# FFN 2's input projection in Strassen's form: seven half-size products in place of eight, with its result kept in DRAM

## The chip, the cores and the metric

One core of a Trainium2 chip runs the whole program. The metric is device time in microseconds (us), the median of three runs. Engines: PE (TensorE: matmul), DVE (VectorE), ACT (ScalarE), POOL (GpSimd), SP (SyncE, which only starts DMAs here). Each engine works through its own instructions in a fixed order, and waits for others through semaphores.

## The reference

One step of a decoder layer on 1056 rows (1024 of a prompt, 32 of samples) with a model width of 1024. The change concerns the last of its three parts, the second FFN:

```python
D_MODEL, D_FF = 1024, 2816

def swiglu_ffn(h, w_in, w_out):
    a, b = jnp.split(h @ w_in, 2, axis=-1)
    return (jax.nn.silu(a) * b) @ w_out

def decoder_layer(...):
    ...                                            # first FFN
    x = x + gt2[:, None, :] * m                    # attention and retention, merged
    h = modulate(x, norm_ffn2, sh3, sc3)           # RMS norm, scale, shift
    x = x + HALF_STEP * gt3[:, None, :] * swiglu_ffn(h, ffn2_w_in, ffn2_w_out)
```

A final RMS norm over x gives the main output. All data are float32.

## The kernel before

Activations lie transposed in SBUF: feature k*128+p on partition p of tile k, the 1056 rows along the free axis, cut into three row blocks `rb` of 352 columns (the last one holds the 32 sample rows too). Every float32 operand of a large product is split in two parts, `h` (rounded) and `l` (the rest), by `split` (L176): ACT copies with rounding, DVE (or POOL, where a weight reader has `eng=G`) subtracts. A product of two such operands is three matmuls, h·h, h·l and l·h (`mm3`, L225 to L230), each with its own 128x128 weights. `hh[k]`, `hl[k]` (k = 0..7) are the split normed input of the part that runs, and `X` (named Y here) is the residual x.

The work is one long program: FFN 1, then retention and attention, the merged output projection `w_out` (matmuls into `wop`, L1321 to L1328), and FFN 2. What sets the order is the order in the code together with a list scheduler that places instructions on their engines; weights are read ahead by SP, as far as buffers are free.

FFN 2 is the call of `ffn` at L1376. The 2816 hidden features are 22 tiles `ft` of 128. `CHUNKS2` puts them in chunks of four (the last of two). For each tile of a chunk the weights `wa{ft}`, `wb{ft}` (1024x128 each) are read and split (one ACT and one DVE instruction of 1024 columns each); then for each row block `pa` = h·wa and `pb` = h·wb are made by 24 matmuls of 352 columns each (`unit`, L242), ACT takes silu of `pa` (L512), DVE multiplies by `pb` (L513), and the product is split into `gh`, `gl` (L514). After a chunk its output projection runs: for each of eight output tiles and three row blocks, 3 x (tiles of the chunk) matmuls of 352 columns into `po`, which DVE adds into x (`residual`, L481). So all of x and all of a chunk's `gh`, `gl` stay in SBUF.

`norm` (L449) for row blocks 0 and 1 runs between the last products of `w_out` (L1328), that of row block 2 inside FFN 2's first tile (`final`, L1331). Its last steps are the splits `hl`, by DVE for even k and by POOL for odd k (L473). At the end `after2` (L1341) makes the final norm and writes the output.

The instruction that the page calls `L179 ... x<-y,yh` is the subtraction of a split; `L172` is its rounding copy.

## Time and profile before

| | |
|---|---|
| median of three runs | 3204.2 us (3199.22 to 3204.82) |
| the profiled execution: its own time | 3204.28 us |
| its span, first to last instruction | 3202.5 us |
| mean granted TensorE clock | 0.986 of 2.4 GHz |
| busy PE / DVE / ACT / POOL | 96% / 53% / 36% / 14% |
| first matmul of FFN 2 / first of its tile 2 | 2412.55 us / 2466.59 us |

Times of rows are microseconds from the span's start. A PE row has the start of a matmul and how long it is in the pipe; since matmuls overlap, the distance between starts (called pitch below) says what one costs. "Idle before <-releaser" names what a late instruction waited for.

### The profile page before, as it was taken

The page shows a single profiled execution, that of the slowest core. Times are in us where ns is not written, and L with a number is a line of the kernel's source. Part 1 is how long each engine was busy: PE and PEld are TensorE (multiplying, and loading weights), DVE is VectorE, ACT ScalarE, POOL GpSimd, SP SyncE. Part 2 cuts the span into 40 slices and gives each one's busy share as a digit, 9 for nine tenths or more (in the row PEclk, how much of TensorE's full clock was granted, in tenths as well). Part 3 has the DMA queues.
Part 4 walks back from the last instruction along what each step waited for, and adds up shares of the span by engine and source line. Part 5 has one row for each costly group of instructions (what it writes and reads, how often), then busy time and mean ns, then how long its engine had stood idle before and what let it go on. Part 6 is the DMA issues. An engine that isn't in the chain of part 4 may idle for free.

```text
span 3202.5 us, 47920 instructions
## 1 busy us (share of the span) xinstructions
PE 3060.3 (96%) x19135; PEld 2925.4 (91%) x19135; DVE 1700.5 (53%) x3683; ACT 1151.3 (36%) x2164; POOL 452.0 (14%) x456
## 2 busy tenths in 40 slices
PE   7999999999999999999999998998999999999998
PEld 4999999999999999988888888988889999999998
DVE  6443434334366666668867777776655323233235
ACT  5422232222234243346555556554444111111113
POOL 2000000000132222212222222223021000000002
PEclk9999999999999999999999999998999999999999
DMA  6232222221131322222221121225622111111111
GB/s 215 61 116 81 80 91 87 86 79 53 52 121 59 100 77 83 89 84 84 75 65 60 56 71 56 73 68 172 202 74 66 47 46 47 47 47 47 47 47 61
DMA packets 261369, 254.18 MB, mean 79 GB/s; under 512 B 13216, under 2 KB 223649, under 8 KB 261146
## 3 DMA queue, kind: packets, MB, share of 16 engines
q1 hardware_dynamic: 245226, 200.38, 20.5%
q0 software_dynamic: 15920, 50.74, 4.5%
...
q14 instruction: 73, 0.60, 0.1%
...
## 4 chain that ended last, share of the span: by engine, by line
PE 39%; DVE 9%; ACT 3%; issue 1%; DMA 1%; POOL 0%; DVEq 0%; SPq 0%; ACTq 0%; POOLq 0%
PE pb L228 3%; PE pa L228 3%; PE pa L229 3%; PE pa L230 3%; PE pb L229 3%; PE pb L230 3%; PE po L228 3%; PE po L229 2%; PE po L230 2%; PE gp L228 1%; PE gp L230 1%; PE gp L229 1%; ACT P L1139 1%; PE at L1163 1%; DVE rao L334 1%
## 5 line engine op out<-in xcount | busy, mean ns | idle before, releaser
L513 DVE TENSOR_TENSOR silu<-silu,pb 128x352 f32<-128x352 f32 x132 | 68.7, 521 | 503.5 <-PE pb L230 501.4
L172 ACT ACTIVATE gh<-silu 128x352 fp32r<-128x352 f32 x132 | 65.2, 494 | 325.4 <-DVE silu L513 325.2
L484 DVE SCALAR_TENSOR_TENSOR Y<-po,mod,Y 128x352 f32<-128x352 f32 (+1 forms) x144 | 82.1, 571 | 123.3 <-PE po L230 123.2
L447 POOL TENSOR_TENSOR acc<-acc,sq 128x352 f32<-128x352 f32 x27 | 29.8, 1103 | 804.7 <-ACT sq L446 795.8
L484 DVE SCALAR_TENSOR_TENSOR X<-po,mod,X 128x352 f32<-128x352 f32 (+1 forms) x144 | 81.7, 570 | 112.1 <-PE po L230 111.6
L512 ACT ACTIVATE silu<-pa 128x352 f32<-128x352 f32 x132 | 60.5, 458 | 205.9 <-PE pa L230 205.8
L1139 ACT ACTIVATE P<-s,mx 128x256 f32<-128x256 f32 (+7 forms) x128 | 94.9, 742 | 80.4 <-DVE mx L1137 72.2
L447 POOL TENSOR_TENSOR accf<-accf,sq 128x352 f32<-128x352 f32 x9 | 8.8, 974 | 726.8 <-ACT sq L446 726.8
L228 PE MATMUL po<-gh,wo_0h 128*128 128x352 f32 x288 | 94.6, 328 | 5.1 <-DVE X L484 4.1
L1137 DVE TENSOR_REDUCE mx<-s 128x1 f32<-128x256 f32 (+7 forms) x128 | 95.5, 752 | 1.8
L229 PE MATMUL po<-gl,wo_0h 128*128 128x352 f32 x288 | 93.8, 326 | 0.0
L230 PE MATMUL po<-gh,wo_0l 128*128 128x352 f32 x288 | 93.7, 325 | 0.0
L179 DVE TENSOR_TENSOR gl<-silu,gh 128x352 fp32r<-128x352 f32 x132 | 69.1, 524 | 46.2 <-ACT gh L172 45.8
L228 PE MATMUL po<-gh,wo_1h 128*128 128x352 f32 x288 | 93.4, 324 | 0.0
L230 PE MATMUL po<-gh,wo_1l 128*128 128x352 f32 x288 | 92.8, 322 | 0.0
L229 PE MATMUL po<-gl,wo_1h 128*128 128x352 f32 x288 | 92.6, 322 | 0.0
L172 ACT ACTIVATE ah<-at 128x512 fp32r<-128x512 f32 (+1 forms) x80 | 44.4, 555 | 98.4 <-PE at L1163 97.7
L228 PE MATMUL po<-gh,wo_3h 128*128 128x352 f32 x240 | 77.5, 323 | 1.2 <-DVE rs L489 1.2
L228 PE MATMUL po<-gh,wo_2h 128*128 128x352 f32 x240 | 77.7, 324 | 0.0
L229 PE MATMUL po<-gl,wo_2h 128*128 128x352 f32 x240 | 77.2, 322 | 0.0
L229 PE MATMUL po<-gl,wo_3h 128*128 128x352 f32 x240 | 77.2, 322 | 0.0
L230 PE MATMUL po<-gh,wo_2l 128*128 128x352 f32 x240 | 77.2, 321 | 0.0
...
## 6 DMA issues: line engine op xcount, KB each, us to landing
...
```

Source lines behind the costliest of these rows:

```text
L172: S.activation(out, in_, AF.Copy, scale=scale)
L179: (eng or V).tensor_tensor(out=l, in0=src, in1=f(h), op=ALU.subtract)
L228: T.matmul(out, wh, xh, start=first and j == 0, stop=False)
L229: T.matmul(out, wh, xl, start=False, stop=False)
L230: behind[0] = T.matmul(out, wl_, xh, start=False, stop=last and j == n - 1).ins
L334: V.scalar_tensor_tensor(out=a[:, j:j + 1], in0=y[:, j:j + 1], scalar=y[:, j:j + 1], in1=h[:, j:j + 1], op0=ALU.mult, op1=ALU.mult)
L447: (V if k % 2 else G).tensor_tensor(out=acc[k % 2], in0=acc[k % 2], in1=sq[:], op=ALU.add)
L484: V.scalar_tensor_tensor(out=x[k][:, c0:c0 + n], in0=p_[:, :n], scalar=gt[:, k, 0:1], in1=x[k][:, c0:c0 + n], op0=ALU.mult, op1=ALU.add)
L512: S.activation(s_[:], pa[:, :RB], AF.Silu)
L513: V.tensor_tensor(out=s_[:], in0=s_[:], in1=pb[:, :RB], op=ALU.mult)
L1137: V.tensor_reduce(out=mx[:], in_=ss[:, :wd], op=ALU.max, axis=AX.X, negate=True)
L1139: S.activation(pt[:, :wd], ss[:, :wd], AF.Exp, bias=mx[:], accum_out=rs[:, c:c + 1])
```

## The change

Twenty of the 22 input tiles of FFN 2 (ft 2 to 21) are computed in Strassen's form (Winograd's variant). The input h is cut in four: features 0..511 and 512..1023 by columns 0..527 and 528..1055; the weights of one tile in four as well: wb and wa, each by its upper and lower 512 features. Instead of eight products of quarters there are seven, with sums of weight quarters (`s1` to `s4`) and of input quarters (`T1` to `T4`) as operands, and the four result quarters are put together from the seven products in PSUM and by DVE and ACT.

- A product is 4 (k) x 3 (h·h, h·l, l·h) x 2 (column halves `s` of 264) = 24 matmuls of 264 columns; a tile has 168 in place of 144 of 352.
- Input sums `T1` to `T3` are made once (`sums`), into new tiles `gx`; `T4` (`last_sum`) takes the place of h's upper right quarter. Each is split again.
- Per tile: seven splits of 512 columns, four sums of 512 on DVE, and ten evictions of 264 columns on each of DVE and ACT. Six PSUM banks, x, q and y times two halves, each single, hold the products: x collects the first, third, fifth and sixth product one upon the other and is read after each, q the fourth and seventh, y the second.
- A tile's product silu(a)·b isn't split into `gh`, `gl`, but stored to DRAM (`gd`, through POOL's queue), and read back at the output projection (`ffn_out`, `gr`, through SP's queue, two buffers) and split there into `hh`, `hl`, which are free by then.
- x is stored to DRAM after each row block of `w_out` (`keep`), since its SBUF is needed for `gx`, and read back (`Z`) ahead of the output projection, which now follows all 22 input tiles.
- Tiles 0 and 1 are made as before (`ffn_plain`), so that `sums` can be made beside them.
- Everywhere in the program, a split whose subtraction is POOL's is cut along its second axis in pieces of two: four of 256 columns for one of 1024.

```diff
     def split(h, l, src, scale=1.0, eng=None):
         acth(h, src, scale)
-        if isinstance(scale, float) and scale == 1.0:
+        if eng is G:
+            for a in range(0, h.shape[1], 2):
+                G.tensor_tensor(out=l[:, a:a + 2, :], in0=src[:, a:a + 2, :], in1=f(h)[:, a:a + 2, :], op=ALU.subtract)
+        elif isinstance(scale, float) and scale == 1.0:
             (eng or V).tensor_tensor(out=l, in0=src, in1=f(h), op=ALU.subtract)
...
+    def sums(ta, gx):
+        def less(a, b, tag, name):
...
+        for k in range(4):
+            b11, b12, b22 = half(k, 0), half(k, 1), half(4 + k, 1)
+            t1 = less(b12, b11, "p1", f"t1_{k}")
+            split(*(x[:] for x in gx[0][k]), t1[:])
+            yield
+            V.tensor_tensor(out=t1[:], in0=f(b22[0]), in1=t1[:], op=ALU.subtract)
+            V.tensor_tensor(out=t1[:], in0=t1[:], in1=f(b22[1]), op=ALU.add)
+            split(*(x[:] for x in gx[1][k]), t1[:])
+            yield
+            split(*(x[:] for x in gx[2][k]), less(b22, b12, "u2", f"t3_{k}")[:])
+            yield
...
+    def ffn_seven(w, ta, gx, win, fts, once, more=iter(()), per=0):
+        operand = [[half(k, 0) for k in range(4)], [half(4 + k, 0) for k in range(4)],
+                   *([(h[:], l[:]) for h, l in gx[c]] for c in (1, 0, 2)),
+                   [half(k, 1) for k in range(4)], [half(4 + k, 1) for k in range(4)]]
+        X_, Q_, Y_ = range(3)
+        home = (X_, Y_, X_, Q_, X_, X_, Q_)
+        opens = (0, 1, 3)
...
+            yield two(a11, "c1")
+            yield two(a12, "c2")
+            s1 = s_(a21, a22, ALU.add, "s1")
+            s2 = s_(s1, a11, ALU.subtract, "s2")
+            yield two(s2, "c6")
+            yield two(s1, "c5")
+            s4 = s_(a12, s2, ALU.subtract, "s4")
+            yield two(s_(a11, a21, ALU.subtract, "s3"), "c7")
+            yield two(a22, "c4")
+            yield two(s4, "c3")
...
+            for j in range(7):
...
+                for s in range(2):
+                    cs_ = slice(s * QR, (s + 1) * QR)
+                    mm3(p[home[j]][s][:, :QR], [(wh[:, k, :], wl_[:, k, :]) for k in range(4)],
+                        [(h[:, cs_], l[:, cs_]) for h, l in operand[j]], first=j in opens, skip_group_check=True)
+                for s in range(2):
...
+                    if j == 0:
+                        S.activation(p1[:, cs_], x, AF.Copy)
+                    elif j == 1:
+                        V.tensor_tensor(out=p1[:, cs_], in0=p1[:, cs_], in1=y, op=ALU.add)
+                    elif j == 2:
+                        S.activation(u2[:, cs_], x, AF.Copy)
+                    elif j == 3:
+                        S.activation(p5[:, cs_], q, AF.Copy)
+                    elif j == 4:
+                        V.tensor_tensor(out=p5[:, cs_], in0=p5[:, cs_], in1=x, op=ALU.add)
+                        S.activation(p5[:, cs_], p5[:, cs_], AF.Silu)
+                    elif j == 5:
+                        S.activation(sa[:, cs_], x, AF.Silu)
+                        V.tensor_tensor(out=p1[:, cs_], in0=p1[:, cs_], in1=sa[:, cs_], op=ALU.mult)
+                    else:
+                        V.tensor_tensor(out=u2[:, cs_], in0=u2[:, cs_], in1=q, op=ALU.add)
+                        V.tensor_tensor(out=u2[:, cs_], in0=u2[:, cs_], in1=p5[:, cs_], op=ALU.mult)
+                if j == 5:
+                    st(out=gd[ft][:, :HR], in_=p1[:])
+                elif j == 6:
+                    st(out=gd[ft][:, HR:], in_=u2[:])
+                next(once, None)
...
+    def ffn_out(w, tp, x, wout, gt, after, chunks, homes, bridge=iter(()), more=iter(())):
+        def stage(ci):
+            for q, ft in enumerate(chunks[ci]):
+                r = tp.tile([P, ROWS], F32, tag="gr", name=f"gr{ft}", bufs=2)
+                ld(out=r[:], in_=gd[ft][:, :])
+                split(*(t[:] for t in homes[ci][q]), r[:])
+                yield
...
+        def keep(rb):
+            st(out=xd[:, rbs(rb)].rearrange("(k p) c -> p k c", p=P), in_=X[:, :, rbs(rb)])
...
-            ffn(s2, w, pool(s2, "t2"), x, i["ffn2_w_in"][0], i["ffn2_w_out"][0], lambda: mods[8], after2, CHUNKS2, 1,
-                pre={(0, 0): final()})
+            todo = back()
+            win2 = i["ffn2_w_in"][0]
+            ffn_plain(w3, tp2, win2, [0, 1], 1, {(0, 0): final()}, todo)
+            for _ in todo:
+                pass
+            psum_seven(1)
+            ffn_seven(w3, gx[3], gx, win2, list(range(2, DFF // P)), last_sum(gx[3], gx))
...
+            ffn_out(w3, pool(s2, "t3"), x, i["ffn2_w_out"][0], lambda: mods[8], after2, CHUNKS2,
+                    [[(hh[c % 2 * 4 + q], hl[c % 2 * 4 + q]) for q in range(4)] for c in range(len(CHUNKS2))])
```

In the rows of the order below a weight name like `c12` is the split quarter sum c1 of tile 2 (`c621`: c6 of tile 21), both of its parts in one tile; `x2_0` is PSUM bank x of tile 2, column half 0.

**PE at the entry to tile 2.** Before, tile 1's last matmul (`wb1`) is followed by tile 2's first:

```order
L229 MATMUL pb1_2_24535<-hl7_121,wb1h_24396 128x352
L230 MATMUL pb1_2_24535<-hh7_113,wb1l_24397 128x352
L228 MATMUL pa2_0_24577<-hh0_106,wa2h_24567 128x352
L229 MATMUL pa2_0_24577<-hl0_114,wa2h_24567 128x352
L230 MATMUL pa2_0_24577<-hh0_106,wa2l_24568 128x352
L228 MATMUL pa2_0_24577<-hh1_107,wa2h_24567 128x352
```

With the change:

```order
L235 MATMUL pb1_2_24789<-hl7_143,wb1h_24641 128x352
L236 MATMUL pb1_2_24789<-hh7_135,wb1l_24642 128x352
L234 MATMUL x2_0_24865<-hh0_128,c12_24879 128x264
L235 MATMUL x2_0_24865<-hl0_136,c12_24879 128x264
L234 MATMUL x2_1_24866<-hh0_128,c12_24879 128x264
L235 MATMUL x2_1_24866<-hl0_136,c12_24879 128x264
L234 MATMUL y2_0_24869<-hh4_132,c22_24882 128x264
L235 MATMUL y2_0_24869<-hl4_140,c22_24882 128x264
L234 MATMUL y2_1_24870<-hh4_132,c22_24882 128x264
L235 MATMUL y2_1_24870<-hl4_140,c22_24882 128x264
L236 MATMUL x2_0_24865<-hh0_128,c12_24879 128x264
L234 MATMUL x2_0_24865<-hh1_129,c12_24879 128x264
```

Tile 2 now begins with the two matmuls that need only the rounded part, for each half of the first two products (c1, c2), and only then comes the l·h matmul (L236), which needs the subtracted part of c1.

**DVE from the end of the norm to that point.** Before, from the last `hl` of the norm on, two weight splits of 1024 columns and the work on tile 0 stand there:

```order
L513 TENSOR_TENSOR silu0_1_24328<-silu0_1_24328,pb0_1_24303 128x352
L476 SCALAR_TENSOR_TENSOR hl6_120<-nt2_6_24264,mod6_4694,hh6_112 128x352
L179 TENSOR_TENSOR gl0_24127<-silu0_1_24328,gh0_24123 128x352
L179 TENSOR_TENSOR wb1l_24397<-wb1r_24394,wb1h_24396 128x1024
L513 TENSOR_TENSOR silu0_2_24383<-silu0_2_24383,pb0_2_24358 128x352
L179 TENSOR_TENSOR wa2l_24568<-wa2r_24565,wa2h_24567 128x1024
L179 TENSOR_TENSOR gl0_24127<-silu0_2_24383,gh0_24123 128x352
L513 TENSOR_TENSOR silu1_0_24450<-silu1_0_24450,pb1_0_24425 128x352
```

With the change `hl6` of row block 2 is followed by 47 rows (42 of 528 columns for the input sums, one weight split of 1024, four `silu` products of 352) before c1 of tile 2, whose last ones are:

```order
L185 TENSOR_TENSOR gl03_24487<-t1_3_24843,gh03_24486 128x528
L572 TENSOR_TENSOR silu1_2_24814<-silu1_2_24814,pb1_2_24789 128x352
L601 TENSOR_TENSOR t1_3_24843<-hh7_135,t1_3_24843 128x528
L593 TENSOR_TENSOR t3_3_24854<-t3_3_24854,t3_3u_24855 128x528
L602 TENSOR_TENSOR t1_3_24843<-t1_3_24843,hl7_143 128x528
L185 TENSOR_TENSOR c12_24879<-wb2r_24875,c12_24879 128x512
L185 TENSOR_TENSOR gl23_24503<-t3_3_24854,gh23_24502 128x528
L185 TENSOR_TENSOR gl13_24495<-t1_3_24843,gh13_24494 128x528
```

The subtraction for `c12`, which had no such work ahead of it, now stands behind nearly all of `sums`.

**DVE within a tile.** Before, tile 17 to 18: 352-column products and splits, and one weight split of 1024 for each half of a tile's weights:

```order
L513 TENSOR_TENSOR silu17_0_28818<-silu17_0_28818,pb17_0_28793 128x352
L179 TENSOR_TENSOR gl1_24128<-silu17_0_28818,gh1_24124 128x352
L513 TENSOR_TENSOR silu17_1_28873<-silu17_1_28873,pb17_1_28848 128x352
L179 TENSOR_TENSOR gl1_24128<-silu17_1_28873,gh1_24124 128x352
L179 TENSOR_TENSOR wb18l_28942<-wb18r_28939,wb18h_28941 128x1024
L513 TENSOR_TENSOR silu17_2_28928<-silu17_2_28928,pb17_2_28903 128x352
L179 TENSOR_TENSOR wa19l_29113<-wa19r_29110,wa19h_29112 128x1024
L179 TENSOR_TENSOR gl1_24128<-silu17_2_28928,gh1_24124 128x352
L513 TENSOR_TENSOR silu18_0_28995<-silu18_0_28995,pb18_0_28970 128x352
```

With the change, from tile 20's second product to its sixth:

```order
L185 TENSOR_TENSOR c420_29150<-wa20r_28977,c420_29150 128x512
L185 TENSOR_TENSOR c320_29179<-s420_29117,c320_29179 128x512
L682 TENSOR_TENSOR p1_20_29113<-p1_20_29113,y20_0_29111 128x264
L644 TENSOR_TENSOR s421_29350<-wb21r_29208,s221_29274 128x512
L682 TENSOR_TENSOR p1_20_29113<-p1_20_29113,y20_1_29112 128x264
L185 TENSOR_TENSOR c121_29212<-wb21r_29208,c121_29212 128x512
L185 TENSOR_TENSOR c221_29241<-wb21r_29208,c221_29241 128x512
L185 TENSOR_TENSOR c621_29276<-s221_29274,c621_29276 128x512
L688 TENSOR_TENSOR p5_20_29115<-p5_20_29115,x20_0_29107 128x264
L644 TENSOR_TENSOR s321_29352<-wb21r_29208,wa21r_29210 128x512
L688 TENSOR_TENSOR p5_20_29115<-p5_20_29115,x20_1_29108 128x264
```

The addition of bank x to `p5` (L688), which frees that bank for the next product, now stands behind two or three splits of later weights.

**SP at the start of the output projection.** Before, an output chunk's weights stood between weights of input tiles:

```order
L197 DMA wb3r_24748<-ffn2_w_in 128x8x128
L197 DMA wo0_0r_24919<-ffn2_w_out 128x4x256
L197 DMA wo0_1r_25015<-ffn2_w_out 128x4x256
L197 DMA wo0_2r_25111<-ffn2_w_out 128x4x256
L197 DMA wo0_3r_25207<-ffn2_w_out 128x4x256
L197 DMA wa4r_25303<-ffn2_w_in 128x8x128
L197 DMA wb4r_25309<-ffn2_w_in 128x8x128
```

With the change:

```order
L203 DMA wb21r_29208<-ffn2_w_in 128x8x128
L203 DMA wa21r_29210<-ffn2_w_in 128x8x128
L203 DMA wo0_0r_29590<-ffn2_w_out 128x4x256
L203 DMA wo0_1r_29690<-ffn2_w_out 128x4x256
L203 DMA wo0_2r_29790<-ffn2_w_out 128x4x256
L203 DMA wo0_3r_29890<-ffn2_w_out 128x4x256
L709 DMA gr0_29574<-gd0_67 128x1056
L709 DMA gr1_29578<-gd1_68 128x1056
L203 DMA wo1_0r_29990<-ffn2_w_out 128x4x256
L709 DMA gr2_29582<-gd2_69 128x1056
L709 DMA gr3_29586<-gd3_70 128x1056
```

The readings of `gd2`, `gd3` wait until the first two buffers `gr` have been split, and stand ahead of all later loads.

## Rows read from the trace of the kernel before

**Rows 1.** From the page: busy time of the engines over the whole span (share of it, number of instructions), and the busy tenths of DVE in 40 slices of 80 us.

```profile
PE 3060.3 (96%) x19135; PEld 2925.4 (91%) x19135; DVE 1700.5 (53%) x3683; ACT 1151.3 (36%) x2164; POOL 452.0 (14%) x456
...
DVE  6443434334366666668867777776655323233235
```

**Rows 2.** Windows (from:to, length, then busy time and number of instructions of PE, PE weight loads, DVE, ACT and POOL, the granted clock, the DMA share and rate): two stretches of 100 us within FFN 2, and the last.

```profile
2500.00:2600.00 100.00, 100.00 (x631) 100.00 (x630) 32.65 (x62) 14.78 (x22) 0.00 (x0) 1.00 0.15 43
2900.00:3000.00 100.00, 100.00 (x630) 100.00 (x630) 33.91 (x64) 15.73 (x23) 0.00 (x0) 1.00 0.18 53
3100.00:3202.50 102.50, 91.40 (x590) 88.79 (x588) 48.30 (x126) 26.52 (x48) 18.79 (x17) 0.94 0.16 58
```

**Rows 3.** What PE waited for from 2440 us to the end (engine, line, releaser: us in all, times, longest).

```profile
PE yt L1363 <- ACT yo L1366: 2.3, 3, 1.8
PE ym L1356 <- POOL accf L447: 1.3, 1, 1.3
PE yt L1363 <- DVE rs L489: 0.4, 1, 0.4
PE pa L229 <- POOL hl L473: 0.3, 1, 0.3
```

**Rows 4.** PE timeline (start, us in the pipe, line, operands): the first matmul of `pa5_2` and the first of `pa6_1`, with the 96 matmuls of 352 columns from the one to the other.

```profile
2596.32 0.32 PE L228 MATMUL pa<-hh,wa5h 128*128 128x352 f32 x1
2611.58 0.32 PE L228 MATMUL pa<-hh,wa6h 128*128 128x352 f32 x1
```

**Rows 5.** PE timeline: the first and the thirteenth of thirteen successive matmuls of 256 columns in a retention chunk, then the first and the sixth of six of 288 columns in attention, all with weights of their own.

```profile
980.77 0.28 PE L228 MATMUL U<-vh,nh 128*128 128x256 f32 x1
...
982.19 0.28 PE L228 MATMUL pro<-ph,vh 128*128 128x256 f32 x1
...
2231.45 0.29 PE L228 MATMUL sc<-kth,qmh 128*128 128x288 f32 x1
...
2232.11 0.29 PE L230 MATMUL sc<-kth,qml 128*128 128x288 f32 x1
```

**Rows 6.** Groups of DVE instructions by line, operation and shape (count, then busy us, mean ns of one, then idle time before them and its releaser): subtractions and products of two float32 tiles of 352, 512, 1024 and 256 columns.

```profile
L513 DVE TENSOR_TENSOR silu<-silu,pb 128x352 f32<-128x352 f32 x132 | 68.7, 521 | 503.5 <-PE pb L230 501.4 <-ACT silu L512 2.1
L179 DVE TENSOR_TENSOR al<-at,ah 128x512 fp32r<-128x512 f32 x48 | 32.9, 686 | 19.4 <-ACT ah L172 19.4
L179 DVE TENSOR_TENSOR wo_1l<-wo_1r,wo_1h 128x1024 fp32r<-128x1024 f32 x12 | 14.7, 1226 | 20.5 <-ACT wo_1h L172 20.5
L561 DVE TENSOR_TENSOR gs<-nh 128x256 f32<-128x256 f32 x16 | 6.7, 422 | 7.4 <-ACT nh L560 7.4
```

**Rows 7.** The same for ACT: copies and squares of 512 and 256 columns.

```profile
L172 ACT ACTIVATE sth<-st 128x512 fp32r<-128x512 f32 x32 | 20.2, 631 | 85.5 <-PE srx L857 77.7 <-DMA st<-state_ret 7.7
L1175 ACT ACTIVATE osq<-o 128x256 f32<-128x256 f32 x32 | 12.2, 382 | 17.2 <-PE o L230 17.0
```

**Rows 8.** DVE timeline at the end of the norm of row block 2 and after it.

```profile
2439.03 0.57 DVE L476 SCALAR_TENSOR_TENSOR hl<-nt,mod,hh 128x352 fp32r<-128x352 f32 x1
2439.78 0.52 DVE L179 TENSOR_TENSOR gl<-silu,gh 128x352 fp32r<-128x352 f32 x1 [0.18 <-ACT gh L172]
```

**Rows 9.** PE timeline: tile 2's first matmul.

```profile
2466.59 0.32 PE L228 MATMUL pa<-hh,wa2h 128*128 128x352 f32 x1
```

**Rows 10.** PE timeline around the one long wait of PE in the `w_out` phase (from 2399.89 to 2402.06 six matmuls start), then the granted clock of the two windows behind it (columns as in rows 2).

```profile
2394.92 0.32 PE L230 MATMUL wop<-hh,wo21l 128*128 128x352 f32 x1
2399.07 1.54 PE L370 MATMUL rsn<-acc,ones 128*128 128x352 f32 x2 [3.83 <-DVE acc L447]
2399.89 1.01 PE L228 MATMUL wop<-hh,wo22h 128*128 128x352 f32 x1
...
2402.06 0.32 PE L228 MATMUL wop<-hh,wo22h 128*128 128x352 f32 x1
...
2399.10:2402.00 2.90, 2.90 (x8) 2.40 (x9) 2.90 (x4) 1.54 (x3) 2.55 (x2) 0.51 0.00 1
2402.00:2412.50 10.50, 10.50 (x68) 10.50 (x67) 9.82 (x16) 6.80 (x13) 3.55 (x4) 1.00 0.35 102
```

**Rows 11.** POOL: groups of subtractions of 512 and 1024 columns (columns as in rows 6), then the DVE timeline while one of 1024 runs on POOL from 1504.95 to 1507.33 us.

```profile
L179 POOL TENSOR_TENSOR rv2al<-rv21r,rv2ah 128x512 fp32r<-128x512 f32 x1 | 1.3, 1277 | 0.0
L179 POOL TENSOR_TENSOR k2l<-k2r,k2h 128x1024 fp32r<-128x1024 f32 x1 | 2.4, 2401 | 0.1
L179 POOL TENSOR_TENSOR v2l<-v2r,v2h 128x1024 fp32r<-128x1024 f32 x1 | 3.0, 3008 | 15.5 <-ACT v2h L172 15.5
1504.95 2.38 POOL L179 TENSOR_TENSOR v1l<-v1r,v1h 128x1024 fp32r<-128x1024 f32 x1 [6.97 <-ACT v1h L172]
1505.07 2.40 DVE L334 SCALAR_TENSOR_TENSOR rao<-ryo,rho 128x1 f32<-128x1 f32 x2
1507.61 0.34 DVE L334 SCALAR_TENSOR_TENSOR rao<-ryo,rho 128x1 f32<-128x1 f32 x2
```

**Rows 12.** What PE waited for most from 1200 to 2000 us (attention).

```profile
PE rqo L364 <- DVE rdo L359: 28.7, 14, 3.3
```

**Rows 13.** DMA issues from 2000 to 2200 us and from 2330 to 2460 us (count, KB each, median us from issue to landing).

```profile
m<-md POOLq DMA_DIRECT2D x3, 352.0 KB, 3.8
Y<-xd POOLq DMA_DIRECT2D x2, 704.0 KB, 5.3
```

More of the change, by code (lines that the diff above doesn't have):

```diff
@@ L21 @@
 P = 128
+HR, QR = 528, 264
 D = 1024
@@ L29 @@
 NRB = 3
+AHEAD = 5
 SC = RB - NS
@@ L144, in build @@
     xd = dr.tile([KT * P, ROWS], F32, name="xd")
+    gd = [dr.tile([P, ROWS], F32, name=f"gd{k}") for k in range(DFF // P)]
     od = [dr.tile([P, SEQ], F32, name=f"od{k}") for k in range(KT)]
@@ new lines, in last_sum @@
+    def last_sum(ta, gx):
+        for k in range(4):
+            b21, t2 = half(4 + k, 0), gx[1][k]
+            t = ta.tile([P, HR], F32, tag="u2", name=f"t4_{k}", bufs=2)
+            u = ta.tile([P, HR], F32, tag="p5", name=f"t4_{k}u")
+            V.tensor_tensor(out=t[:], in0=f(b21[0]), in1=f(t2[0][:]), op=ALU.subtract)
+            V.tensor_tensor(out=u[:], in0=f(b21[1]), in1=f(t2[1][:]), op=ALU.subtract)
+            V.tensor_tensor(out=t[:], in0=t[:], in1=u[:], op=ALU.add)
+            split(*half(k, 1), t[:])
+            yield
```

141 lines of the change are left out of this document (131 added, 10 removed).

## The prediction

> **What bounds the kernel now.** I read the page's busy times first: PE is busy 96% of the span, DVE 53% [rows 1]. Then the windows of FFN 2: in stretches of 100 us PE is busy for all 100, at the full granted clock of 2.4 GHz, with 630 or 631 matmuls, while DVE works a third of the time and POOL not at all [rows 2]. Then the waits: from 2440 us to the end PE waits 4.3 us in all, nearly all of it in the final norm [rows 3]. So in FFN 2 the time is the number of matmuls times what one costs, and an engine beside PE matters only where it comes late.
>
> What one costs is read as pitch. 96 matmuls of 352 columns take 2611.58 - 2596.32 = 15.26 us [rows 4], 158.9 ns each. Twelve of 256 columns take 1.42 us (118.3 ns each), five of 288 take 0.66 us (132 ns) [rows 5]. Each has weights of its own, and yet (158.9 - 118.3) / 96 = 0.423 ns a column is all that more columns cost, about one cycle of 2.4 GHz; the row of 288 lies on the same line (131.9). At 264 columns it passes at 121.7; I take 122 ns.
>
> **The sum.** It is made against the profiled execution, 3204.3 us, which is the median within 0.1 us; 0.2% (6.4 us) is what a measurement here can tell from no change.
>
> *Products.* Twenty tiles had 20 x 144 = 2880 matmuls of 352 columns: 2880 x 158.9 ns = 457.6 us. Now they have 20 x 168 = 3360 of 264: 3360 x 122 ns = 409.9 us. **-47.7 us.** Bounds by the rows on both sides: -60.1 at 118.3 ns, -14.1 at 132. The row of 256 is the nearer one. The other 1584 + 288 matmuls of FFN 2 stay as they are.
>
> Against this speaks a figure in the Trainium skill, "TensorE: Matmul & The Clock Gate", section "Back-to-back issue gap": sustained spacing of 81 ns at 128 columns and 131 at 512, so 0.13 ns a column; an estimate by it gives 110 ns at 352 and 99 at 264, and the products would cost some 16 us more than before, not 48 less. The trace disagrees: 159 and 118 ns stand 41 ns apart over 96 columns [rows 4, 5], and the measurement decides.
>
> *DVE and ACT within a tile.* A tile's 168 matmuls take 20.5 us. DVE has 11 instructions of 512 (0.686 us) and 10 of 264 (0.43, a little over the 256 row), 11.9 us [rows 6]; ACT 7 of 512 and 10 of 264, 8.3 us [rows 7]. Neither is the bound. The tightest place is bank x between the fifth and the sixth product, which follow each other in one bank. DVE's addition of that bank to `p5` stands behind the split of the next c6, and this waits for a weight slot that the fourth product gives back. From the fifth product's start: ACT copy 0.39, ACT rounding 0.63, DVE subtraction 0.69, addition 0.43, so 2.14 us. The bank's first half is wanted at 24 x 0.122 = 2.93. 0.8 us are left, so I charge **0**; the upper end is a rival below.
>
> *Entry to tile 2.* In the kernel before DVE ends the norm with `hl6` at 2439.6 and is then nearly free [rows 8]; tile 2 begins on PE at 2466.59 [rows 9]. Now 47 instructions stand between `hl6` and the subtraction of c1: 42 of 528 columns at 0.708 (on the line between the rows of 512 and 1024), one of 1024 at 1.23, four of 352 at 0.52, then c1's own 0.69 [rows 6]: 33.7 us, ready at 2473.3. None of the 352 ones waits for PE, since each `pb` is done earlier than DVE gets there. PE can do 8 matmuls without it (1.0 us), so it waits 2473.3 - 2467.6 = 5.7. Going on in both orders: c6 of tile 2 is 0.9 late, tile 3's early c2 2.4 (tile 2's splits and T4's 16 additions share DVE), and T4's last part 2.2, at about 2504. Sum **+11.3 us**; bounds 6 (only the first) and 18 (DVE 20% slower on its 34 us).
>
> After its one long wait of 3.83 us the granted clock was 0.51, the lower level of 1.2 GHz, for 2.9 us, and then 1.00: six matmuls took 2.17 us where 0.95 is normal [rows 10]. One such stretch follows here: **+1.2 us.**
>
> *Exit.* The output projection needs gd0 to gd3 split. The first two are read ahead, but the subtraction to `hl0` stands behind tile 21's last results on DVE, and ends about 0.65 us after the last product, `hl1` 1.7 later (1056 columns at 1.26). `gr2` starts only when `gr0` has been split. Its landing isn't shown; copies of 352 KB and 704 KB from DRAM land in 3.8 and 5.3 us [rows 13], so 528 KB in about 4.5. With ACT and DVE behind it, `hl2` and `hl3` come 7 to 10 us after the last product, where PE has only 36 matmuls (5.7 us) to do. **+4.5 us**, bounds 2 and 10, and one more stretch at the low clock, **+1.2**. Later chunks are read 45 us ahead (288 matmuls), and hide. Z's eight loads are wanted by DVE's first residual only, some 7 us after the last product; three have been issued by the seventh product. I charge nothing; if they come late, PE first fills its three output banks, and that is in the upper bound.
>
> *Norm.* `keep(2)` stores x from POOL's queue among the sums of squares of row block 2; it waits for the last residual, and POOL's next addition stands behind it. **+1.0 us**, bounds 0 and 2, since PE's wait for the last `hl` was barely hidden (0.3 us) [rows 3].
>
> *POOL's pieces.* About 40 splits of 1024 and 60 of 512 become pieces of 256. By the rows of 512 and 1024 (1.28 and 2.40) a column costs 2.2 ns and a start 0.16 us, so four pieces take 0.5 us more than one. In attention a DVE pair that takes 0.34 us took 2.40 while POOL ran a split of 1024 [rows 11]; with pieces DVE would get between them. PE waits 28.7 us for `rdo`, which ends that DVE chain [rows 12]: a gain of a quarter of it, 8 us, is the one end; 8 us lost through later weights, a fifth of the 100 splits by 0.4 us each, is the other. I take **0**: most of these waits fall where POOL is idle, and the splits are wanted far later.
>
> *Storing and reading* gd (2 x 22 x 0.54 MB) and x (2 x 4.3 MB) moves 32 MB more in FFN 2's 750 us, 43 GB/s on top of 43 to 53 at 15% to 18% of the DMA engines [rows 2]: nothing.
>
> Sum: -47.7 + 11.3 + 1.2 + 4.5 + 1.2 + 1.0 = -28.5; 3204.3 - 28.5 = **3176 us**.
>
> **The rivals.**
>
> *A, slower: bank x holds PE up in every tile.* The 2.14 us above are a chain of four instructions with no semaphore time and no stray DVE instruction. If it is longer by 0.8 us it begins to cost; a stop of 1.4 us a tile takes the whole gain away (20 x 1.4 = 28), and 1.7 makes it slower than can be measured. One split of 512 (0.69) and one eviction (0.43) ahead of it, and two more ACT instructions of 0.6, would be 2.3 too much, a stop of 1.5. At 2 us a tile: 3176 + 40 = 3216. For it: single banks, and DVE's order puts three splits before the addition. Against: DVE and ACT are 58% and 40% busy. 0.07 for slower, 0.08 for a partial stop of about 1 us (3196).
>
> *B, slower: fewer columns don't pay.* At the 132 ns of the 288 row it is -14.1 + 19.2, 3209 us; at 457.6 / 3360 = 136 ns the products cost what they did, 3223. Against it stand both rows. 0.02. This is where the skill's figure above would lead, with some 3239 by its estimate.
>
> *C, entry and exit cost twice as much*: ACT's splits of `sums` and DVE alternate and each waits for the other, or Z and `gr` come late: +14, 3190. 0.13.
>
> *D, POOL's pieces free the chain in attention*: -8 to -10, 3167. For: rows 11 and 12. Against: DVE must happen to have its short instructions just then. 0.10.
>
> *E, the change doesn't do what it says*: were the weight load not hidden, the pitch would not fall. The skill's "TensorE: Matmul & The Clock Gate", section "Part 3: Packing small matmuls — row/col tiling", says a weight load overlaps a matmul only in another row group, and every matmul here uses all rows. The trace shows 100 us of weight loads beside 100 us of matmuls [rows 2], so the load is hidden at 159 ns. Folded into B.
>
> **How the numbers follow.** Forecast 0.60; A 0.07 and 0.08, B 0.02, C 0.13, D 0.10. Faster by over 0.2% (under 3197.9): forecast, C, D and half of A's partial case, 0.87. Slower by over 0.2% (above 3210.6): 0.08 with A and B; 0.05 between. The range leaves out A's and B's slow ends and D's far end: 3160 (D with the products at 118 ns would be 3156) to 3200.
>
> **What would show it.** Right: 168 matmuls of a tile in 20.5 us, PE busy 100 of 100 us in the tiles; one wait of 5 to 6 us for `c12` near 2468, some of 1 to 3 us up to 2505; waits for `hl2`, `hl3` of 4 to 5 us at the start of the output; FFN 2 shorter by 29 and the stretch up to 2412 unchanged. Wrong: a repeated wait of PE for `p5` at the sixth product (A), a pitch above 130 ns (B), waits for `gx` or Z beyond 20 us (C), a start of FFN 2 earlier or later by over 5 us (D).

## The result and the profile after

The changed kernel takes 3172.9 us (median of 4 runs, 3166.6 to 3174.9) against 3202.8 (4 runs, 3199.2 to 3204.8) beside it: ratio 0.9904 [0.9887, 0.9922], by which 30.7 us are off, between 25 and 36. 3176 was forecast. The profiled execution took 3172.2 us with a span of 3170.4, 32.1 shorter than the span before. First the page's busy times and the DVE row of its 40 slices:

```profile
PE 3019.7 (95%) x19615; PEld 2880.9 (91%) x19615; DVE 1862.1 (59%) x4019; ACT 1241.8 (39%) x2376; POOL 523.6 (17%) x696
...
DVE  6443434344366666667877777776558755554555
```

Beside [rows 1]: 480 matmuls more and yet 41 us less of PE; DVE goes from 53% to 59%, most of it in the last ten slices. Next the windows (columns as in [rows 2]): the start of the seven-product tiles, its two stretches at a lower clock, the steady tiles, the start of the output projection, one of its two stretches at the lower clock, and its steady part.

```profile
2458.72:2495.00 36.28, 31.44 (x226) 29.97 (x226) 32.69 (x58) 14.37 (x30) 1.63 (x3) 0.92 0.24 72
2462.30:2465.40 3.10, 3.10 (x14) 3.10 (x15) 3.10 (x6) 0.46 (x3) 0.00 (x0) 0.50 0.02 5
2493.03:2497.00 3.97, 3.97 (x21) 3.97 (x22) 2.57 (x5) 1.66 (x4) 0.54 (x1) 0.61 0.17 68
2500.00:2600.00 100.00, 100.00 (x822) 100.00 (x821) 54.26 (x104) 37.92 (x82) 5.42 (x10) 1.00 0.27 81
2878.13:2892.94 14.81, 9.80 (x38) 8.62 (x36) 7.29 (x8) 4.33 (x4) 2.15 (x5) 0.77 1.00 366
2889.00:2892.10 3.10, 3.04 (x10) 3.04 (x11) 1.27 (x2) 0.46 (x1) 0.00 (x0) 0.50 1.03 393
3000.00:3100.00 100.00, 100.00 (x627) 100.00 (x626) 51.29 (x102) 15.62 (x15) 0.00 (x0) 1.00 0.19 59
```

PE is busy for the whole of the steady tiles; what is lost lies at both ends, where it waits and then runs at the lower clock. The 822 matmuls counted in 100 us take in those that reach over the window's edges; the pitch is read from the first matmuls of tiles 5 and 6, 168 matmuls of 264 columns apart:

```profile
2529.63 0.28 PE L234 MATMUL x<-hh,c 128*128 128x264 f32 x1
...
2550.13 0.28 PE L234 MATMUL x<-hh,c 128*128 128x264 f32 x1
```

These 20.50 us are 122.0 ns each, as was taken, and tiles 4 to 21 all take 20.50 us. What PE waited for from 2380 to 3170 us (columns as in [rows 3]):

```profile
PE po L234 <- ACT hh L175: 3.6, 2, 1.8
PE rsn L376 <- DVE acc L453: 3.5, 1, 3.5
PE pa L235 <- POOL hl L479: 3.0, 2, 2.3
...
PE x L234 <- ACT hh L175: 2.0, 1, 2.0
PE x L236 <- DVE c L185: 1.5, 1, 1.5
PE po L235 <- DVE hl L185: 1.4, 2, 0.9
```

The `x` rows are the entry to tile 2 (`hh` there is T4), the `po` rows the exit. Nothing in the list falls between 2495 and 2878 us: no tile waits for bank x. The `pa` row is the wait for the norm's last splits in tile 0. The 0.3 us in [rows 3] are only its part behind 2440 us; from 2412.5 to 2466 us the kernel before waits 3.1 us in all, of which `hl` is 1.2:

```profile
PE pa L229 <- POOL hl L473: 1.2, 3, 0.7
PE pb L228 <- DVE rs L489: 1.2, 1, 1.2
PE pa L230 <- DVE wa0l L179: 0.6, 1, 0.6
```

So the wait for `hl` went from 1.2 to 3.0 us, while the other two vanished.

By stages, from the first and last matmuls of each (us, profiled executions):

| stage | before | after | difference | forecast |
|---|---|---|---|---|
| up to FFN 2's first matmul | 2412.6 | 2406.0 | -6.5 | 0 |
| from there to tile 2 | 54.0 | 52.7 | -1.3 | +1.0 |
| twenty tiles | 457.6 | 419.4 | -38.2 | -35.2 |
| last product to the end of 36 output matmuls | 5.7 | 14.8 | +9.1 | +5.7 |
| from there to the end, and the rest | | | +4.8 | 0 |

The twenty tiles are 20 x 20.50 = 410.0 us, 47.6 less than before, and 9.4 of loss in tiles 2 and 3 (25.32 and 25.09 us). PE's timeline (start, us in the pipe, line, operands, idle before) at tile 2's first wait, at T4, and from the last product on:

```profile
2459.84 0.39 PE L234 MATMUL x<-hh,c 128*128 128x264 f32 x1 [0.73 <-DVE silu L572]
...
2462.30 0.59 PE L236 MATMUL x<-hh,c 128*128 128x264 f32 x1 [1.46 <-DVE c L185]
2462.69 0.42 PE L234 MATMUL x<-hh,c 128*128 128x264 f32 x1
2462.91 0.42 PE L235 MATMUL x<-hl,c 128*128 128x264 f32 x1
...
2491.30 0.51 PE L234 MATMUL x<-hh,c 128*128 128x264 f32 x2 [1.97 <-ACT hh L175]
...
2878.01 0.28 PE L236 MATMUL q<-hh,c 128*128 128x264 f32 x1
2880.11 0.42 PE L234 MATMUL po<-hh,wo_0h 128*128 128x352 f32 x1 [1.81 <-ACT hh L175]
2881.40 0.43 PE L235 MATMUL po<-hl,wo_0h 128*128 128x352 f32 x1 [0.87 <-DVE hl L185]
...
2887.77 0.75 PE L234 MATMUL po<-hh,wo_0h 128*128 128x352 f32 x3 [1.78 <-ACT hh L175]
2889.07 0.66 PE L235 MATMUL po<-hl,wo_0h 128*128 128x352 f32 x1 [0.55 <-DVE hl L185]
```

After 1.46 us of idling the matmuls start 0.22 us apart, at the lower level of 1.2 GHz, until 2465.4. At the exit both pairs of readings are late, gr0 and gr1 too, which the prediction took to be in place. Of the 9.1 us there 5.0 are idle time; most of the rest is two stretches at the lower clock, from 2882 to 2885 us and from 2889 to 2892. ACT's timeline names the releaser:

```profile
2878.97 1.08 ACT L175 ACTIVATE hh<-gr 128x1056 fp32r<-128x1056 f32 x1 [2.21 <-DMA gr<-gd]
2880.63 1.08 ACT L175 ACTIVATE hh<-gr 128x1056 fp32r<-128x1056 f32 x1 [0.58 <-DMA gr<-gd]
2886.64 1.08 ACT L175 ACTIVATE hh<-gr 128x1056 fp32r<-128x1056 f32 x1 [4.92 <-DMA gr<-gd]
```

gr0 was issued at 2871.39, and the copy that waits for it starts 7.6 us later, where 4.5 was taken for the landing. Z's eight loads went out from POOL's queue from 2870.07, 2877.11 and 2884.19 on; from 2871 to 2879 us the DMA engines were busy 94% of the time (344 GB/s), and behind that all the time (share 1.00, 366 GB/s).

### The profile page after: what moved, and what is told of

Same layout as the page of the kernel before. It is cut to its first block, busy times and chain, and to the rows that moved or that the text cites. A ratio compares the mean times of both kernels' runs of the same rounds, so it can differ in the third digit from the quotient of the medians.

```text
span 3170.4 us, 49976 instructions
## 1 busy us (share of the span) xinstructions
PE 3019.7 (95%) x19615; PEld 2880.9 (91%) x19615; DVE 1862.1 (59%) x4019; ACT 1241.8 (39%) x2376; POOL 523.6 (17%) x696
## 4 chain that ended last, share of the span: by engine, by line
PE 37%; DVE 9%; ACT 4%; DMA 2%; issue 1%; POOL 1%; DVEq 0%; ACTq 0%; POOLq 0%; SPq 0%
PE x L234 2%; PE x L236 2%; PE x L235 2%; PE po L234 2%; PE po L235 2%; PE po L236 2%; PE gp L234 1%; PE gp L236 1%; PE gp L235 1%; PE q L234 1%; PE q L235 1%; PE q L236 1%; DVE rao L340 1%; PE wop L234 1%; PE wop L236 1%
## 5 line engine op out<-in xcount | busy, mean ns | idle before, releaser
L490 DVE SCALAR_TENSOR_TENSOR Z<-po,mod,Z 128x352 f32<-128x352 f32 (+1 forms) x144 | 81.5, 571 | 94.0 <-PE po L236 93.8
L234 PE MATMUL x<-hh,c 128*128 128x264 f32 x320 | 92.5, 290 | 2.9 <-ACT hh L175 2.0
L236 PE MATMUL x<-hh,c 128*128 128x264 f32 x320 | 91.9, 288 | 1.5 <-DVE c L185 1.5
L235 PE MATMUL x<-hl,c 128*128 128x264 f32 x320 | 92.2, 288 | 0.2 <-DVE hl L185 0.2
L235 PE MATMUL x<-gl,c 128*128 128x264 f32 x320 | 91.1, 285 | 0.0
L234 PE MATMUL x<-gh,c 128*128 128x264 f32 x320 | 91.1, 285 | 0.0
L236 PE MATMUL x<-gh,c 128*128 128x264 f32 x320 | 90.9, 285 | 0.0
L1342 PE MATMUL s<-kk,st 128*128 128x512 f32 (+2 forms) x192 | 68.4, 358 | 0.5 <-ACT P L1348 0.5
L234 PE MATMUL gp<-hh,g_0h 128*128 128x352 f32 x192 | 65.5, 341 | 0.0
L234 PE MATMUL gp<-hh,g_1h 128*128 128x352 f32 x192 | 65.3, 340 | 0.0
L1343 PE MATMUL s<-kl,st 128*128 128x512 f32 (+2 forms) x192 | 64.4, 347 | 0.4 <-ACT kl L1308 0.3
L234 PEld LDWEIGHTS x<-hh,c 128*128 128x128 f32 x320 | 61.3, 192 | 3.6 <-ACT hh L175 2.2
```

What stands on the lines that cost most here:

```text
L234: T.matmul(out, wh, xh, start=first and j == 0, stop=False, **kw)
L235: T.matmul(out, wh, xl, start=False, stop=False, **kw)
L236: behind[0] = T.matmul(out, wl_, xh, start=False, stop=last and j == n - 1, **kw).ins
L490: V.scalar_tensor_tensor(out=x[k][:, c0:c0 + n], in0=p_[:, :n], scalar=gt[:, k, 0:1], in1=x[k][:, c0:c0 + n], op0=ALU.mult, op1=ALU.add)
L1342: T.matmul(ss[:, a:e], s_[:, qc], k_[:, a:e], start=True, stop=False)
L1343: T.matmul(ss[:, a:e], s_[:, qc], l_[:, a:e], start=False, stop=True)
```

## The experiments

Each was timed beside the kernel before on its chip; ratios are to that one. The changed kernel's own interval is 0.9887 to 0.9922; of the kernels built on it only the last two, with several edits at once, have intervals clear of that. What a single step at the entry or the exit is worth is read from the stretch that it alters, in one profiled execution each.

**The pieces alone.** The kernel before, with only POOL's splits cut in pieces of 256 columns:

```diff
         acth(h, src, scale)
-        if isinstance(scale, float) and scale == 1.0:
+        if eng is G:
+            for a in range(0, h.shape[1], 2):
+                G.tensor_tensor(out=l[:, a:a + 2, :], in0=src[:, a:a + 2, :], in1=f(h)[:, a:a + 2, :], op=ALU.subtract)
+        elif isinstance(scale, float) and scale == 1.0:
```

> The kernel before with one part of the change alone: subtractions on POOL cut in pieces of 256 columns. Theory 1 (pieces let DVE's short instructions of attention through): PE waits less for `rdo` and `sdm`, the stretch up to FFN 2 gets shorter by 6 to 12 us, the first matmul of FFN 2 at 2401 to 2407 us for 2412.6, the whole at about 3194. Rival (the 6.5 us by which FFN 2 began earlier come from the w_out phase, where the change moves the stores of x and the weight buffers): no shift, 3203 +- 2.

3195.0 us, ratio 0.9972 [0.9962, 0.9982]: 9 us less, between 6 and 12. The instructions `rao` on DVE, of the chain that rival D had in mind, first of the kernel before, then with pieces (ns min/median/max; first and last start; shapes):

```profile
L334 DVE SCALAR_TENSOR_TENSOR rao<-ryo,rho x192: 200/213/2346, 1505.1 to 2180.1; 128x1 f32<-128x1 f32 x192
...
L337 DVE SCALAR_TENSOR_TENSOR rao<-ryo,rho x192: 199/213/792, 1503.2 to 2166.2; 128x1 f32<-128x1 f32 x192
```

Most are not held at all (the medians stay), and the longest hold falls from one whole split to one piece. The mean of `rao` even rises (235 to 286 ns): shorter holds, but more of them. PE's wait for `rdo` went only from 37.0 to 34.8 us between 1420 us and `w_out`; all its waits there went from 73.2 to 65.0 (that for `P` before the attention product from 7.4 to 4.1; others rose and fell). What fell most on DVE are two groups of 320 columns, `M` and `gv`. First `M` before, then with pieces, and last the windows from 1420 us to `w_out`, in the same order:

```profile
L1215 DVE SCALAR_TENSOR_TENSOR M<-gt,gv 128x320 f32<-128x320 f32 x8 | 14.6, 1825 | 0.0
L1218 DVE SCALAR_TENSOR_TENSOR M<-gt,gv 128x320 f32<-128x320 f32 x8 | 4.7, 581 | 0.0
...
1420.00:2252.30 832.30, 759.36 (x4766) 712.40 (x4767) 615.25 (x1672) 450.35 (x927) 218.36 (x208) 0.97 0.27 83
1420.00:2235.50 815.50, 751.03 (x4766) 701.62 (x4767) 605.86 (x1672) 449.49 (x926) 241.82 (x322) 0.98 0.27 85
```

Six of the eight `M` stand beside a split on POOL: 2.1 to 2.4 us each before, 0.5 to 0.65 with pieces, and 0.47 to 0.49 for the two that stand beside none. The same 1672 instructions keep DVE busy 9.4 us less. Of the 16.8 us by which the stretch is shorter, 8.2 are waits of PE, and 8.3 less busy time of PE for the same 4766 matmuls, at a higher granted clock. The profiled execution, 3187.6 us, is the shortest of ten, so these say where rather than how much. Where is plain: matmul by matmul it leads the kernel before by 0.2 us at 1412 us, by 12.4 at 1937, and by 16.2 at 2288.

**All but the pieces.** The change with POOL's subtractions whole:

```diff
-        if eng is G:
-            for a in range(0, h.shape[1], 2):
-                G.tensor_tensor(out=l[:, a:a + 2, :], in0=src[:, a:a + 2, :], in1=f(h)[:, a:a + 2, :], op=ALU.subtract)
-        elif isinstance(scale, float) and scale == 1.0:
+        if isinstance(scale, float) and scale == 1.0:
```

> The changed kernel with whole subtractions on POOL again. Theory 1: the first matmul of FFN 2 goes back by 6 us or more, from 2406 to 2412 or later, since without the gain in attention the w_out phase keeps its loss of about 5 us; about 3180 to 3184 for 3173. Rival: FFN 2 still starts at 2406, 3173.

3182.3 us, 0.9934 [0.9917, 0.9950]. So FFN 2's form alone gives 21 us [16, 27]. The pieces give 9 us by the run before and 9.6 as the difference from the change, whose interval touches this one; 21 + 9 is within 1 us of the 30.7 measured. FFN 2 starts at 2412.8 in the profile, as before. That start alone proves little: it lies between 2405.3 and 2412.3 in the profiles of the seven kernels whose code up to there is the change's. Again the difference arises in attention: from the 8500th to the 11500th matmul the change gains 9.8 us on this kernel, and the same 1644 DVE instructions from the 8500th matmul to the 13200th last 695.9 us in all here and 685.7 in the change (kernel before: 695.1; pieces alone: 685.8).

**Pieces of 512.** As the first, with four blocks a piece:

```diff
-            for a in range(0, h.shape[1], 2):
+            for a in range(0, h.shape[1], 4):
```

> The kernel before with POOL's subtractions of 1024 columns cut in two pieces of 512 and those of 512 whole (pieces of 256 throughout gave a ratio of 0.9972). Theory 1 (DVE's instructions are held for the length of one POOL instruction): with pieces of half the length about half of the gain, 3200, PE's waits from 1420 us to the start of `wop` about 69 us for 73 before and 65 with pieces of 256. Rival (any cut gives the whole gain): 3196 and 65 us.

3198.9 us, 0.9993 [0.9981, 1.0005]: no gain that can be told from none, but half the gain (0.9986) lies in the interval too, so the time doesn't decide between the two theories. PE's waits in the same stretch sum to 71.3 us, 1.9 less than before where pieces of 256 gave 8.2. On DVE the 1644 instructions last 696.2 us, no less than before: the `M` above falls only two thirds as far (to 998 ns), and what it gives back other instructions lose, `rao` 7.2 us, `rho`, `gas` and `gbs` 6 to 7 each. So it is only with pieces of 256 that DVE is held less in all.

**x read behind gd.** Z's loads move from POOL's queue to SP's, behind the first chunk's `gr`:

```diff
         run(stage(0))
+        z_load()
...
-            for k in range(KT):
-                st(out=x[k], in_=xd[k * P:(k + 1) * P, :])
+            def z_load():
+                for k in range(KT):
+                    ld(out=x[k], in_=xd[k * P:(k + 1) * P, :])
```

> The changed kernel with x read back (Z) behind gd0 and gd1 on SP's queue, two pieces of it ahead of gd2 and gd3 and six behind, instead of on POOL's queue from the fourth product of tile 21 on. Theory 2 (the wait at the exit is a transfer that shares its bandwidth with Z): gd0 and gd1 land some 3 to 4 us after their issue instead of 7.6 to 9, the wait for them vanishes, and the stretch from the last product to the 36th output matmul, 14.2 us now, falls to 9 or 10; 3168. Rival (the waits are set by the chain behind two buffers, issue, ACT, DVE, whatever else is read): within 1 us of 14, 3173.

3167.0 us, 0.9882 [0.9862, 0.9901]. The first output matmul starts 0.12 us behind the last product, so the wait for gr0 and gr1 was Z's traffic. Two of Z's loads still go out ahead of gr2 and gr3. The waits for that pair remain, and from the last product to the end of the 36 matmuls it is 13.4 us (14.8 in the change).

**Four buffers.** The same, with four `gr`, so that gr2 needn't wait for gr0's split:

```diff
-                r = tp.tile([P, ROWS], F32, tag="gr", name=f"gr{ft}", bufs=2)
+                r = tp.tile([P, ROWS], F32, tag="gr", name=f"gr{ft}", bufs=4)
```

> The changed kernel with x read back behind gd0 to gd3 on SP's queue, and four buffers for gd instead of two, so that gd2 and gd3 wait for no split. Theory 5 (two causes at the exit, each hidden behind the other: bandwidth shared with Z, and the two buffers): from the last product to the 36th output matmul 7 to 9 us, for 14.7 in the changed kernel and 13.2 with Z later alone; about 3165. Rival (ACT and DVE, 1.1 and 1.3 us for each of the four splits, are what PE waits for): 11 us or more.

3165.5 us, 0.9878 [0.9861, 0.9894]; that stretch is 9.4 us. PE's waits at the exit (2860 to 2910 us) are down to

```profile
PE po L234 <- ACT hh L175: 1.5, 1, 1.5
PE po L235 <- DVE hl L185: 0.8, 2, 0.6
```

So the exit had two causes, traffic and buffers. The first is shown by removal. With four buffers all four readings also stand ahead of all of Z's loads, so this run took away the rest of the traffic together with the limit of two buffers; how much each of these gave isn't separated.

**Three plain tiles.** Tile 2 is left in the plain form, so that DVE has a tile more for its sums:

```diff
-            ffn_plain(w3, tp2, win2, [0, 1], 1, {(0, 0): final()}, todo)
+            ffn_plain(w3, tp2, win2, [0, 1, 2], 1, {(0, 0): final()}, todo)
...
-            ffn_seven(w3, gx[3], gx, win2, list(range(2, DFF // P)), last_sum(gx[3], gx))
+            ffn_seven(w3, gx[3], gx, win2, list(range(3, DFF // P)), last_sum(gx[3], gx))
```

> The changed kernel with three plain tiles ahead (0 to 2) and nineteen of seven products. Theory 3 (at the entry PE waits because the sums are not ready in two tiles' time): with 22.9 us more ahead of them the sums are covered, the 10.5 us lost in the first tile of seven products fall to 2 or less, and the plain tile costs 144 x 158.9 - 168 x 121.7 = 2.4 us more than one of seven products: 6 us faster in all, 3167. Rival (the loss is that of DVE's and ACT's whole load in any first tile, weights and T4 included): the loss stays above 7 us, 3173 or slower.

3171.7 us, 0.9896 [0.9880, 0.9913]. Nineteen tiles take 391.4 us, where 19 x 20.50 are 389.5: the loss falls from 9.4 to 1.9. Less the 2.4 us that tile 2 no longer saves (47.6 / 20) some 5 should be left; the time from FFN 2's start to PE's end is shorter by 2.4, and the total cannot be told from the change.

**More reads of bank x.** Two, and then six, additions of 264 columns ahead of the one to `p5` for the first half:

```diff
                     elif j == 4:
+                        for _ in range(2 if s == 0 else 0):
+                            V.tensor_tensor(out=more_[:], in0=p1[:, cs_], in1=x, op=ALU.add)
```

> The changed kernel with two more DVE reads of bank x (264 columns, 0.35 us apart) ahead of the addition that frees its first half after the fifth product, in all twenty tiles; the results stay as they are. Theory 6 (0.8 us of slack there, as the prediction has it): 0.7 us fit, no wait of PE, the twenty tiles take 419 to 421 us as now. Rival (less slack, or none): 4 us or more.

> The same with six more reads, 2.1 us. Theory 6: 2.1 - 0.8 = 1.3 us of wait at the sixth product of each tile, 26 us in all, PE's waits for `p5` at L234, about 3199. Rival (PE has other work to put ahead, so that the wait is less): under 10 us.

With two: 3174.7 us, 0.9909 [0.9893, 0.9926], and the twenty tiles take 420.9 us. With six: 3176.5 us, 0.9911 [0.9894, 0.9927], tiles 422.7. 26 us were expected by the theory of a fixed order for six; 3.3 came, a steady tile taking 20.69 us for 20.50. The window of the kernel with six, then the DVE timeline of a tile with two (its fifth product starts on PE at 2644.57 us):

```profile
2500.00:2600.00 100.00, 100.00 (x814) 99.35 (x813) 64.62 (x134) 37.77 (x82) 5.42 (x10) 1.00 0.26 81
...
2646.32 0.42 DVE L690 TENSOR_TENSOR more<-p,x 128x264 f32<-128x264 f32 x1
2646.66 0.69 DVE L644 TENSOR_TENSOR s<-wb11r,wa11r 128x512 f32<-128x512 f32 x1
2647.26 0.42 DVE L690 TENSOR_TENSOR more<-p,x 128x264 f32<-128x264 f32 x1
2647.60 0.76 DVE L691 TENSOR_TENSOR p<-p,x 128x264 f32<-128x264 f32 x2
```

PE's rows show no idle time. But in both kernels the order has changed: in place of 24 matmuls of the sixth product and then 24 of the seventh, five of the seventh (bank q) stand ahead of the sixth with two reads, and with six reads some ahead of each half of it. With two reads a weight sum of 0.69 us has also slipped in among them, so that the first half is free 3.45 us after the fifth product's start, later than the 2.93 at which the old order wants it; the five matmuls fill most of that, and a steady tile takes 20.60 us. The list scheduler thus filled the gap. So neither run tells what a stop at bank x costs, nor whether 0.7 us fit; the slack itself is read from the change's own tile. Its fifth product starts on PE at 2623.36 us and its sixth at 2626.30; between, ACT and DVE did this:

```profile
2623.56 0.39 ACT L686 ACTIVATE p<-q 128x264 f32<-128x264 f32 x1 [1.02 <-PE q L236]
2623.85 0.62 ACT L175 ACTIVATE c<-s 128x512 fp32r<-128x512 f32 x1
2624.51 0.69 DVE L185 TENSOR_TENSOR c<-s,c 128x512 fp32r<-128x512 f32 x1 [2.24 <-ACT c L175]
2625.12 0.42 DVE L688 TENSOR_TENSOR p<-p,x 128x264 f32<-128x264 f32 x1
```

The addition ends at 2625.54, 2.18 us after the product's start (2.14 forecast), and the bank is wanted at 2.94: 0.76 us of slack. In tiles 3 to 21 it is the same within 0.02 us.

**Weights above x.** In the third branch's w_out phase the weights' pool changes places with x's:

```diff
+            xp = pool(xs2, "x2")
             w2 = W(xs2, 2, 3)
-            xp = pool(xs2, "x2")
```

> The changed kernel with one line moved: the pool of x for the w_out phase is opened ahead of that phase's weight pool, as in the kernel before, so that the first weights land in the memory that they had there. Theory 4 (the 16 us won in attention by the pieces are lost again at the start of the w_out phase, because the weights' place in memory is now one that POOL's stores still read from, and the first weight load waits for them): the first `wop` matmul goes from 2254 back to about 2236, the first of FFN 2 from 2406 to 2396 to 2398, about 3164. Rival (the loss there comes from the stores of x and the new order behind them): `wop` stays at 2254, 3173.

3168.9 us, 0.9887 [0.9871, 0.9904]. In the change PE waits 6.5 us for the first weight `wo0h`, a wait that isn't there before; its load was issued at 2243.98 us. Here it is issued at 2236.48 and that wait is gone; `w_out` starts 9.5 us earlier, FFN 2 only 2.0, which is less than that start differs among profiles. So the place of the weights in memory made the load late, as theory 4 has it; that POOL's stores still read there isn't shown by itself. Most of what it cost is given back before FFN 2.

**The last `hl` on DVE.** In the last norm the last block's subtraction moves from POOL to DVE:

```diff
+        last_norm = sh == 6
...
-                G.tensor_tensor(out=l_, in0=t[:], in1=f(h_), op=ALU.subtract)
+                (V if last_norm and rb == NRB - 1 and k == KT - 1 else G).tensor_tensor(out=l_, in0=t[:], in1=f(h_), op=ALU.subtract)
```

> The changed kernel with the last subtraction of the norm of row block 2 (`hl7`) on DVE, ahead of the input sums, instead of on POOL. Theory 7 (PE's 2.4 us wait for `hl` in tile 0 comes from POOL's subtraction running beside DVE's sums, 2.87 us instead of 0.95, behind a store of tile 0): the waits of PE for `hl` fall from 3.0 us to under 1, tile 2 starts 2 us earlier, about 3171. Rival (the norm as a whole is late, so that PE waits for whatever comes last): the wait moves to the DVE subtraction, no gain, 3173.

3169.4 us, 0.9898 [0.9883, 0.9913]. PE's wait for `hl` goes from 3.0 to 0.6 us, and the way from FFN 2's start to tile 2 from 52.7 to 49.2. What had held it up, in the change (timelines of POOL and DVE):

```profile
2425.89 1.11 POOL L479 TENSOR_TENSOR hl<-nt,hh 128x352 fp32r<-128x352 f32 x1 [1.84 <-ACT hh L175]
2427.78 0.57 POOL L573 DMA_DIRECT2D gd<-silu  x1 [0.78 <-DVE silu L572]
2428.37 2.87 POOL L479 TENSOR_TENSOR hl<-nt,hh 128x352 fp32r<-128x352 f32 x1
...
2427.90 0.70 DVE L591 TENSOR_TENSOR t<-hh 128x528 f32<-128x528 f32 x1
2428.52 0.70 DVE L592 TENSOR_TENSOR t_0u<-hl 128x528 f32<-128x528 f32 x1
2429.14 0.70 DVE L591 TENSOR_TENSOR t<-hh,hh 128x528 f32<-128x528 f32 x1
2429.76 0.70 DVE L593 TENSOR_TENSOR t<-t,t_0u 128x528 f32<-128x528 f32 x1
```

The same subtraction takes 2.87 us while DVE runs the sums back to back, and 1.11 just ahead (all eleven others of this norm take 0.95 to 1.30); and it stood behind the storing of tile 0's `gd`.

**All mended, with two and with three plain tiles.** Four buffers and x read later, weights above x, the last `hl` on DVE; then tile 2 plain as well (edits as above).

> The changed kernel with four things: x's pool opened ahead of the weights in the w_out phase, x read back behind gd0 to gd3, four buffers for gd, and `hl7` of row block 2 on DVE. If the causes found are separate ones the gains add: 2 to 4 us at `wop`, 5.4 at the exit, 2 in the norm, so some 10 us under the changed kernel's 0.9904 of before: a ratio of 0.987 or less. If each gives way to the next wait: 0.988 to 0.989.

> The same with three plain tiles ahead instead of two. By the profile of that edit alone FFN 2 gets 2.4 us shorter (7.6 less lost in the first tile, 2.4 to 2.9 more for the plain tile, and noise): 0.0008 to 0.0016 of the time below the kernel with four edits. Rival: with `hl7` on DVE the sums are later, and two tiles cover no less: the same time.

3159.2 us, 0.9862 [0.9847, 0.9877], and 3150.3, 0.9842 [0.9827, 0.9858]. The second is the fastest of all, some 20 us under the change by the ratios (0.0062 of 3203). It loses 0.8 us in its seven-product tiles (8.5 with two plain tiles), and the 36 matmuls end 7.5 us after the last product; of the waits around the entry (2395 to 2520 us) these are left:

```profile
PE pa L235 <- POOL hl L480: 0.6, 1, 0.6
PE x L234 <- ACT hh L175: 0.3, 1, 0.3
```

## Why the prediction was right, and where it was not

*Products: right.* -47.6 us against -47.7. The pitch went by columns, as the two rows of 352 and 256 said [rows 4, 5]. The sustained spacing in the Trainium skill, "TensorE: Matmul & The Clock Gate", section "Back-to-back issue gap" (81 ns at 128 columns, 131 at 512), isn't what this kernel shows at 264: 122.0 ns.

*In the tile: right*, 0.76 us of slack against 0.8.

*Entry: near in the sum (9.4 against 12.5) by luck, not in its parts.* DVE's work from `hl6` to c1 took 34.3 us as forecast (33.7), but because two errors met: the sums start 0.62 us apart though each lasts 0.70, so 42 of them, priced at 0.708, cost 3.7 us less, and DVE idled 4.5 us among them: 2.6 for ACT's rounding of `wb1`, 0.6 for that of a sum, and 1.2 for PE's `pb`, which the prediction had ruled out. (On the line between 512 and 1024 columns, 528 lie at 0.703, and the four lateness terms add up to 11.2, not 11.3.) And counted from `hl6`, PE came to tile 2 3.8 us later than assumed, 3.0 of it its wait for `hl7`: it waited 1.5 us for c1 in place of 5.7, after 0.7 at a bank that by the trace DVE's last `silu` product still held. With T4's 2.0 and twice 0.2 the waits are 4.6 us in place of 11.3, and the other 4.8 are mostly slow running, in two stretches at the lower clock, in place of 1.2 for one. The three plain tiles show that the place was right: with a tile more of time the loss is 1.9.

*Exit: right place, term too small* (9.1 against 5.7). The step that failed is "I charge nothing" for Z: its loads took the DMA engines from `gr`, for which ACT waited 7.6 us instead of 4.5. The waits came to 5.0 us, close to the 4.5 forecast, but only by luck: 2.7 of them are for gr0 and gr1, which were to be in place. The other 4.1 are slow running, mostly two stretches at the lower clock, where one was charged at 1.2. Moving Z took 14.8 us to 13.4; four buffers, with all of Z behind them, to 9.4.

*Norm: wrong in its parts.* +1.0 was put on `keep(2)`. The wait for `hl` did grow, from 1.2 to 3.0 us, but from a POOL subtraction that stood behind the store of tile 0 and ran beside DVE's sums; the waits for `rs` and `wa0l` (1.8 us) vanished, and the stretch got 1.3 us shorter. The prediction saw only the last 0.3 us of the old waits for `hl`, as its rows begin at 2440. The Trainium skill, "GPSIMD Engine Reference", section "1. Specifications", has POOL and VectorE share their way into SBUF, with contention when a VectorE instruction has two inputs there; the 2.87 us beside the sums agree.

*Pieces: wrong.* 0 was charged and -9 came; rival D had the size, but not the chain. The step that failed is to take 0 because "most of these waits fall where POOL is idle". They do: POOL works during 1.3 of the 37.0 us for which PE waits for `rdo` before. But a wait tells where a delay ends, not where it arose, and DVE as a whole is held 9 to 10 us less with the pieces, in both pairs of kernels. The waits for `rdo`, which D had named, gave only 2 of it in the profile, and `rao` is held longer in all (38.0 to 47.9 us); what fell are `M` and `gv`. By which chains this reaches PE isn't shown.

*Not in the sum:* +4.8 us behind the exit. The output's matmuls run at 627 per 100 us, where FFN 2 before had 630 or 631 (1.6 us over 257), and from the start of PE's last matmul to the end there are 9.1 us, 7.5 before. Why is open; the fastest kernel has 627 too.

So FFN 2's form gave 21 us where 28.5 was forecast, the pieces 9 where 0 was, and the forecast was 3 us off by two misses that met: the closeness of the total is luck. That no tile waited (A), the pitch held (B) and entry and exit cost not twice (C: 18.5 us against 18.2) is settled by the windows and the stage times; A's price of a stop was never seen.
